# Modulation columns by TensorE, x loaded first, and unread products between the first transposes

## Chip, cores and metric

One Trainium2 chip, one of its cores. The metric is the device time of the whole program in microseconds (us). Times inside the program come from one profiled execution of it.

## What is computed

Two layers of a diffusion backbone over 1024 latent and 256 context tokens of width 1024, all in float32. Every sub-layer normalizes its input and modulates it with a shift and a scale that are worked out from a conditioning vector:

```python
mod_lat = (silu_c @ ada_w[i] + ada_b[i])[:, None, :]
sh1, sc1, g1, sh2, sc2, g2 = jnp.split(mod_lat, 6, axis=-1)
h = modulate(rms_norm(x, norm_g[i, 0]), sh1, sc1)        # h * (1 + sc1) + sh1
y = chunk_mlp(h, a_w_in[j], ...)                         # layer 0: gelu(h @ w_in), gating, @ w_out
x = x + g1 * rms_norm(y, norm_g[i, 1])
h = modulate(rms_norm(x, norm_g[i, 2]), sh2, sc2)
x = x + g2 * rms_norm(conv_ffn(h, ...), norm_g[i, 3])
```

Layer 1 has windowed attention in the place of `chunk_mlp`. The change touches only the first line above and the two behind it, for layer 0 and the first five latent tiles: `sh1`, `sc1`, the normalization, and the first quarter of `h @ w_in`.

## The kernel before

Tokens are handled in tiles of 128. The first pass takes five latent tiles (`LAT`). Its start, the **head**, is written out by hand at the end of the quoted code: the instructions of VectorE (`V`), ScalarE (`S`), TensorE (`T`) and the DMA queue of SyncE (`Q`) between `pins.update` and `pins.clear` stay in the order in which they are written. Instructions behind the head, and those of POOL (`G`), are placed by a scheduler.

The head works through the width of 1024 in eight **chunks** of 128 columns. For each chunk k:

- the shift and scale of the chunk are needed as two **columns** of 128 values. `AdaBlock` loads that slice of `ada_w` (two halves of 1024 x 128 for one chunk, or x 256 for two chunks), `accum` multiplies its eight row blocks by the conditioning vector and sums them on VectorE, `total` sums over partitions with products with ones on TensorE, and `finish` adds the bias and the norm's weight (three small operations on VectorE);
- `flip_x(k)` transposes the five scaled tiles of x into a psA bank (five transposes). The scaling (`rstd_of` and the line behind it) takes a square on ScalarE, two small operations on POOL and one scaling on VectorE for each tile;
- `x_hi(k)` applies the columns on ScalarE (two `ACTIVATE`) and casts the result to the high part (one `CAST`); `x_lo(k)` takes the low part on VectorE;
- `w_load`, `w_hi`, `w_lo` load a tile of `w_in` for two chunks and split it in the same way;
- `head_mm(k, part)` is one **group** of five products of 128x512; three parts for each chunk, 24 groups in all, accumulate in four psB banks and one psA bank.

The blocks are one chunk wide for chunks 0 and 1 and two wide for 2-3, 4-5 and 6-7. Loaded slices sit in six `act` buffers, weight tiles in three `raw` buffers. Behind the head the raw buffers are a **ring** that weight tiles of `w_in` and rows of `ada_w` for the next modulations take in turn: a load starts when the tile before it in its buffer has been read by VectorE. There are two psA banks; during the head one of them holds a sum of products. Behind the head, transposes for `lncols` and the two `cwcols` (constants for later) go through psA too, and VectorE copies them out.

At profile time nearly every instruction carries line 50, that of a helper which records all operations, so instructions are told apart by engine and by the tiles that they write and read (`psB<-wh,big`: a product into a psB tile from a weight's high part and a big tile).

Of the kernel before, what the change touches and what calls it, by code (L numbers as in the profile page):

```python
# [10 lines left out]
F32 = mybir.dt.float32  # L11
# [4 lines left out]
P = 128  # L16
D = 1024
KD = D // P
# [14 lines left out]
def hybrid_kernel(  # L33
# [164 lines left out]
    def finish_cols(l, m, s, p, ks):  # L198
        dst = mod_cols(l, m, s)[:, ks]
        V.tensor_tensor(out=dst, in0=p, in1=abcols[:, 48 * l + 8 * m:48 * l + 8 * m + 8][:, ks], op=ALU.add)  # L200
        if m in (1, 4):
            o = 32 * l + (0 if m == 1 else 16)
            V.scalar_tensor_tensor(out=dst, in0=dst, scalar=1.0, in1=ngcols[:, o:o + 8][:, ks],
                                   op0=ALU.add, op1=ALU.mult)
# [122 lines left out]
    def src_row(stage, t):  # L327
        if stage == 0:
            return x_in[0, t * P:(t + 1) * P, :] if t < 8 else ctx_in[0, (t - 8) * P:(t - 7) * P, :]
        return xs[stage][t * P:(t + 1) * P, :]  # L330
# [254 lines left out]
    pA0 = psA()  # L585
    pl0 = [psB() for _ in range(4)] + [pA0[:, 0, :]]

    class AdaBlock:
        def __init__(self, k0, nk):
            self.k0, self.nk = k0, nk  # L590
# [28 lines left out]
                             start=True, stop=True)  # L619

        def finish(self):
            k0, nk = self.k0, self.nk
            p = pts[k0][:, 1, 256:256 + 2 * nk]
            for s in (1, 0):
                finish_cols(0, s, 0, p[:, s * nk:(s + 1) * nk], slice(k0, k0 + nk))

    raws, w0, pts, tms = {}, {}, {}, {}

    def w_load(u, nb=0):
        raws[nb, u] = t_raw()  # L630
        Q.dma_start(raws[nb, u].rearrange("p (a b) -> p a b", a=2),
                    w_in[0][u * 256:u * 256 + 2 * P, E + nb * 512:E + nb * 512 + 512]
                    .rearrange("(k p) n -> p k n", p=P))

    def w_hi(u, nb=0):
        hi, lo = t_w("wh"), t_w("wl")
        w0[nb, u] = (hi.rearrange("p (a b) -> p a b", a=2), lo.rearrange("p (a b) -> p a b", a=2))
        S.copy(hi, raws[nb, u])
        raws[nb, u] = (raws[nb, u], hi, lo)

    def w_lo(u, nb=0):
        raw, hi, lo = raws.pop((nb, u))
        V.tensor_sub(lo, raw, hi)

    def flip_x(k):
        pts[k] = psA()
        for i in range(5):
            T.transpose(out=pts[k][:, i // 4, (i % 4) * P:(i % 4 + 1) * P], in_=xn0[:, i, k * P:(k + 1) * P],
                        identity=ident)

    def x_hi(k):
        pt, tm = pts[k], t_tmp()
        gg, sh = mod_cols(0, 1, 0)[:, k:k + 1], mod_cols(0, 0, 0)[:, k:k + 1]
        S.activation(tm[:, 0:512], pt[:, 0, :], AF.Identity, bias=sh, scale=gg)
        S.activation(tm[:, 512:640], pt[:, 1, 0:128], AF.Identity, bias=sh, scale=gg)
        S.copy(hk(hb0, 0, k)[:, 0:640], tm[:, 0:640])
        tms[k] = tm

    def x_lo(k):
        V.tensor_sub(hk(hb0, 1, k)[:, 0:640], tms[k][:, 0:640], hk(hb0, 0, k)[:, 0:640])  # L660
# [12 lines left out]
        V.tensor_copy(cl, p)  # L673
        return cl

    b0 = AdaBlock(0, 1)
    adab, aR = load_rows([ada_b.rearrange("l (k p) -> (l k) p", p=P)])
    ngr, nR = load_rows([norm_g.rearrange("l i (k p) -> (l i k) p", p=P)])
    for i, t in enumerate(LAT):
        Q.dma_start(xn0[:, i, :], src_row(0, t))  # L680
    w_load(0)
    b1 = AdaBlock(1, 1)
    abcols = cols_in(adab, aR, "abcols")
    ngcols = cols_in(ngr, nR, "ngcols")
    b0.accum(range(KD))
    for i, t in enumerate(LAT):
        r = rstd_of(xn0[:, i, :])
        V.tensor_scalar(out=xn0[:, i, :], in0=xn0[:, i, :], scalar1=r, scalar2=None, op0=ALU.mult)
    flip_x(0)
    b0.total()  # L690
    w_hi(0)
    b0.finish()
    x_hi(0)
    w_lo(0)
    flip_x(1)
    b1.accum(range(0, 4))
    x_lo(0)
    b2 = AdaBlock(2, 2)
    head_mm(0, 0)
    b1.accum(range(4, 8))  # L700
    b1.total()
    b2.accum(range(0, 2))
    b1.finish()
    head_mm(0, 1)
    head_mm(0, 2)
    x_hi(1)
    b2.accum(range(2, 4))
    w_load(1)
    b3 = AdaBlock(4, 2)
    flip_x(2)  # L710
    x_lo(1)
    w_hi(1)
    b2.accum(range(4, 7))
    head_mm(1, 0)
    head_mm(1, 1)
    w_lo(1)
    b2.accum(range(7, 8))
    b2.total()
    head_mm(1, 2)
    b3.accum(range(0, 1))  # L720
    b2.finish()
    x_hi(2)
    b3.accum(range(1, 3))
    x_lo(2)
    w_load(2)
    b4 = AdaBlock(6, 2)
    flip_x(3)
    x_hi(3)
    b3.accum(range(3, 5))
    x_lo(3)  # L730
    w_hi(2)
    head_mm(2, 0)
    head_mm(2, 1)
    head_mm(2, 2)
    flip_x(4)
    head_mm(3, 0)
    b3.accum(range(5, 7))
    w_lo(2)
    b3.accum(range(7, 8))
    head_mm(3, 1)  # L740
    b3.total()
    b4.accum(range(0, 1))
    b3.finish()
    head_mm(3, 2)
    x_hi(4)
    b4.accum(range(1, 3))
    x_lo(4)
    w_load(3)
    flip_x(5)
    x_hi(5)  # L750
    b4.accum(range(3, 5))
    x_lo(5)
    head_mm(4, 0)
    head_mm(4, 1)
    head_mm(4, 2)
    flip_x(6)
    w_hi(3)
    head_mm(5, 0)
    head_mm(5, 1)
    b4.accum(range(5, 8))  # L760
    b4.total()
    w_lo(3)
    b4.finish()
    head_mm(5, 2)
    x_hi(6)
    x_lo(6)
    w_load(0, 1)
    flip_x(7)
    x_hi(7)
# [1351 lines left out]
```

## Time and profile before

| what | us |
|---|---|
| median of three runs | 2856.6 |
| lowest and highest of them | 2850.05, 2860.5 |
| profiled execution, its own time | 2860.88 |
| span of the profiled execution | 2859.1 |

| first 66 us of that execution | us |
|---|---|
| first product of the head | 23.08 |
| last product of the head | 65.07 |

In the timeline a row has the start in us, the duration, the engine, the line, the operation with its output and inputs, how many such instructions were merged, and in brackets how long the engine stood idle before it and what released it. A merged row's duration runs from the first start to the last end. Ends of products are modelled, so the pitch of two starts is the better measure of their cost.

### The profile page before, as it was taken

Reading aid. Unit: us, or ns where it says so; the run is one execution under the profiler, and the core shown is the slowest. Engines: PE = TensorE matmul, PEld = TensorE weight load, DVE = VectorE, ACT = ScalarE, POOL = GpSimd, SP = SyncE. Lnnn points to the kernel's source line nnn. Section 1 sums busy time; section 2 is a strip of 40 time slices with the busy share of each in tenths; the row PEclk is TensorE's granted clock in tenths of the full one; section 3 lists DMA queues with packets and bytes.
Section 4 is the critical chain, followed back from the end, with each engine's and each line's share of the span. In section 5 each row is a group of like instructions: output and inputs, shape, how many; then the busy total and the mean of one; then the engine's idle time right before and its main releaser. Section 6 shows DMA issues by size and latency. Waiting matters only on the chain.

```text
span 2859.1 us, 40314 instructions
## 1 busy us (share of the span) xinstructions
PE 2741.8 (96%) x14570; PEld 2354.1 (82%) x14570; DVE 2221.8 (78%) x3466; ACT 1391.2 (49%) x2291; POOL 616.6 (22%) x806
## 2 busy tenths in 40 slices
PE   7999999999989999999999899999998999999998
PEld 5798887898889888888788778888887888888786
DVE  6567684787779899887776568898887788888776
ACT  4333242232367444455434545777876444445433
POOL 1164021360210212111000124543333121220000
PEclk9999999999999999999999999999999999999999
DMA  7775457554488355467855565347577345545753
GB/s 260 251 234 166 145 161 227 177 167 131 171 249 240 103 170 162 157 217 238 287 169 184 188 212 186 115 145 239 181 242 220 126 162 182 160 144 198 248 177 125
DMA packets 436335, 537.13 MB, mean 188 GB/s; under 512 B 20004, under 2 KB 300452, under 8 KB 436135
## 3 DMA queue, kind: packets, MB, share of 16 engines
q1 hardware_dynamic: 379575, 470.84, 51.4%
q10 hardware_dynamic: 55408, 59.52, 6.2%
q0 software_dynamic: 1152, 4.19, 0.4%
q8 instruction: 115, 1.88, 0.3%
q14 instruction: 85, 0.70, 0.1%
HBM read 414.40 MB, written 120.07 MB: 187 GB/s over the span
## 4 chain that ended last, share of the span: by engine, by line
PE 65%; DVE 13%; DMA 11%; ACT 5%; issue 4%; POOL 2%; SPq 1%; ACTq 0%; DVEq 0%; POOLq 0%
PE psB L50 48%; PE psA L50 16%; DVE row L50 3%; DVE wl L50 3%; DMA raw<-in_ada_w_dram 3%; DVE tmp L50 1%; DVE acc L50 1%; ACT wh L50 1%; ACT tmp L50 1%; DMA xT<-row 1%; DMA raw<-in_a_w_in_dram 1%; DVE y L50 1%; POOL sm L50 1%; DMA raw<-in_f_w_up_dram 1%; DMA raw<-in_f_w_down_dram 1%
## 5 line engine op out<-in xcount | busy, mean ns | idle before, releaser
L50 PE MATMUL psB<-cmb,wh 128*128 128x512 f32 (+2 forms) x2584 | 750.3, 374 | 7.2 <-ACT row L50 6.2
L50 PEld LDWEIGHTS psB<-cmb,wh 128*128 128x128 f32 x2584 | 471.9, 188 | 98.4 <-ACT row L50 8.1
L50 PE MATMUL psB<-cmb,wl 128*128 128x512 f32 (+2 forms) x1292 | 483.2, 374 | 0.2 <-DVE wl L50 0.2
L50 ACT CAST wh<-raw 128x1024 fp32r<-128x1024 f32 (+1 forms) x313 | 265.1, 863 | 441.6 <-PE psB L50 165.5
L50 DVE TENSOR_TENSOR wl<-raw,wh 128x1024 fp32r<-128x1024 f32 (+1 forms) x313 | 307.6, 997 | 106.6 <-ACT wh L50 104.9
L50 PEld LDWEIGHTS psB<-cmb,wl 128*128 128x128 f32 x1292 | 243.2, 188 | 44.0 <-DVE wl L50 0.8
L50 PE MATMUL psB<-wh,big 128*128 128x512 f32 x816 | 271.1, 398 | 3.7 <-ACT big L50 1.3
L50 ACT CAST wh<-row 128x1024 fp32r<-128x1024 f32 (+1 forms) x196 | 162.5, 834 | 186.8 <-DVE row L50 92.3
L50 PE MATMUL psB<-wh,act 128*128 128x512 f32 x640 | 200.1, 390 | 0.8 <-DVE tmp L50 0.8
L50 DVE TENSOR_TENSOR wl<-row,wh 128x1024 fp32r<-128x1024 f32 (+1 forms) x196 | 185.2, 948 | 12.2 <-ACT wh L50 11.8
L50 PE MATMUL psA<-big,wh 128*128 128x320 f32 x1024 | 193.2, 310 | 0.3 <-ACT row L50 0.3
L50 POOL TENSOR_TENSOR row<-raw,raw 128x512 f32<-128x512 f32 x44 | 68.5, 1558 | 574.2 <-DMA raw<-in_f_w_up_dram 490.8
L50 PEld LDWEIGHTS psB<-wh,big 128*128 128x128 f32 x816 | 154.3, 190 | 39.9 <-ACT tmp L50 2.4
L50 DVE SCALAR_TENSOR_TENSOR acc<-raw,ccols,acc 128x1024 f32<-128x1024 f32 x98 | 126.7, 1311 | 75.8 <-DMA raw<-in_ada_w_dram 75.5
L50 DVE SCALAR_TENSOR_TENSOR row<-row,cwcols,row 128x1024 f32<-128x1024 f32 (+2 forms) x142 | 152.6, 1075 | 39.2 <-ACT row L50 22.7
L50 ACT CAST ah<-raw 128x1024 fp32r<-128x1024 f32 x80 | 77.6, 974 | 201.6 <-PE psB L50 80.8
L50 DVE TENSOR_TENSOR row<-row,row 128x512 f32<-128x512 f32 (+4 forms) x169 | 155.9, 926 | 19.9 <-DMA row<-actd 12.2
L50 POOL TENSOR_SCALAR row<-row,sm,sm 128x128 f32<-128x128 f32 x160 | 144.1, 919 | 115.2 <-DMA row<-vscr 99.3
L50 PEld LDWEIGHTS psA<-big,wh 128*128 128x128 f32 x1024 | 159.9, 188 | 0.7 <-ACT row L50 0.5
L50 PE MATMUL psB<-wl,big 128*128 128x512 f32 x408 | 157.2, 395 | 0.9 <-DVE wl L50 0.9
L50 DVE TENSOR_TENSOR al<-raw,ah 128x1024 fp32r<-128x1024 f32 x80 | 90.2, 1128 | 71.9 <-ACT ah L50 71.6
L50 PE MATMUL psB<-row,wh 128*128 128x256 f32 x744 | 136.9, 286 | 8.2 <-ACT wh L50 6.7
(279 smaller groups left out, 6226.0 us busy)
## 6 DMA issues: line engine op xcount, KB each, us to landing
raw<-in_f_w_up_dram SPq DMA_DIRECT2D x121, 512.0 KB, 4.8
raw<-in_ada_w_dram SPq DMA_DIRECT2D x88, 512.0 KB, 4.4
raw<-in_a_w_in_dram SPq DMA_DIRECT2D x64, 512.0 KB, 4.8
wh<-woscr SPq DMA_DIRECT2D x48, 512.0 KB, 4.1
row<-actd SPq DMA_DIRECT2D x44, 512.0 KB, 5.5
actc<-row SPq DMA_DIRECT2D x44, 512.0 KB, 4.1
raw<-actc SPq DMA_DIRECT2D x40, 512.0 KB, 3.6
actd<-row SPq DMA_DIRECT2D x39, 512.0 KB, 2.7
```

The costliest lines, as they stand in the source:

```text
L50: ins = fn(*a, **kw)
```

## The change

`AdaBlock` for chunks 0 and 1, and the first half of the block of 2-3, give way to four `AdaColumn`. An `AdaColumn` loads the two slices of one chunk in two DMAs of 512 KB and needs no sums on VectorE: `total` makes each of the two columns by eight products that accumulate, with the slice as the stationary operand and a column of the conditioning vector as the moving one. Chunks 4-5 and 6-7 keep `AdaBlock`. The loads of x move ahead of the first modulation columns. Three products of ones, whose result is not read, stand ahead of each of the five transposes of chunk 0. The cast of the first weight tile is cut in two halves and moves behind `x_hi(0)`. The written order of the head changes with all this.

```diff
+    class AdaColumn:
+        def __init__(self, k0):
+            self.k0, self.nk, self.rv = k0, 1, {}
             for s in (1, 0):
+                self.rv[s] = t_act((P, KD, P), F32)
+                Q.dma_start(self.rv[s], ada_w[0, :, s * D + k0 * P:s * D + (k0 + 1) * P]
+                            .rearrange("(k p) n -> p k n", p=P))
+
+        def total(self):
+            p = pts[self.k0][:, 1, 256:258]
+            for s in (1, 0):
+                for k in range(KD):
+                    T.matmul(p[:, s:s + 1], self.rv[s][:, k, :], ccols[:, k:k + 1], start=(k == 0), stop=(k == KD - 1))
...
-        S.copy(hi, raws[nb, u])
+        for c in ((0, 512), (512, 1024)) if (nb, u) == (0, 0) else ((0, 1024),):
+            S.copy(hi[:, slice(*c)], raws[nb, u][:, slice(*c)])
...
         for i in range(5):
+            for _ in range(3 if k == 0 else 0):
+                T.matmul(pA0[:, 1, :], ones_r, ones_r.unsqueeze(1).to_broadcast([P, 4, P]), start=True, stop=True)
             T.transpose(out=pts[k][:, i // 4, (i % 4) * P:(i % 4 + 1) * P], in_=xn0[:, i, k * P:(k + 1) * P],
...
-    b0 = AdaBlock(0, 1)
     adab, aR = load_rows([ada_b.rearrange("l (k p) -> (l k) p", p=P)])
     ngr, nR = load_rows([norm_g.rearrange("l i (k p) -> (l i k) p", p=P)])
     for i, t in enumerate(LAT):
         Q.dma_start(xn0[:, i, :], src_row(0, t))
+    b0 = AdaColumn(0)
     w_load(0)
-    b1 = AdaBlock(1, 1)
+    b1 = AdaColumn(1)
+    b2 = AdaColumn(2)
...
-    b0.accum(range(KD))
...
     b0.total()
-    w_hi(0)
     b0.finish()
     x_hi(0)
+    w_hi(0)
+    x_lo(0)
     w_lo(0)
+    b3 = AdaColumn(3)
+    w_load(1)
+    head_mm(0, 0)
     flip_x(1)
...
+    b4.accum(range(4, 8))
+    w_hi(2)
     flip_x(4)
     head_mm(3, 0)
-    b3.accum(range(5, 7))
+    head_mm(3, 1)
+    b4.total()
+    b4.finish()
+    x_hi(4)
     w_lo(2)
...
     flip_x(5)
     x_hi(5)
-    b4.accum(range(3, 5))
     x_lo(5)
+    b6.accum(range(2, 5))
     head_mm(4, 0)
     head_mm(4, 1)
     head_mm(4, 2)
     flip_x(6)
     w_hi(3)
+    b6.accum(range(5, 8))
     head_mm(5, 0)
+    b6.total()
+    b6.finish()
+    x_hi(6)
+    w_lo(3)
+    x_lo(6)
     head_mm(5, 1)
-    b4.accum(range(5, 8))
-    b4.total()
-    w_lo(3)
-    b4.finish()
     head_mm(5, 2)
-    x_hi(6)
-    x_lo(6)
```

Three places as the built programs have them. First POOL at the start of the program; `mask` is a constant for the attention of layer 1, `sm` and `rstT` are the two small operations of each tile's scaling. Before:

```order
L50 MEMSET lead_194 128x16
L50 MEMSET mask 128x640
L50 AFFINE_SELECT mask<-mask 128x384 x2
L50 TENSOR_SCALAR sm_157<-sm_157 128x1
L50 TENSOR_TENSOR rstT<-sm_157,mhalf 128x1
L50 TENSOR_SCALAR sm_163<-sm_163 128x1
L50 TENSOR_TENSOR rstT<-sm_163,mhalf 128x1
```

And now:

```order
L50 TENSOR_SCALAR sm_147<-sm_147 128x1
L50 MEMSET lead_221 128x16
L50 MEMSET mask 128x640
L50 TENSOR_TENSOR rstT<-sm_147,mhalf 128x1
L50 AFFINE_SELECT mask<-mask 128x384
L50 TENSOR_SCALAR sm_153<-sm_153 128x1
L50 TENSOR_TENSOR rstT<-sm_153,mhalf 128x1
L50 AFFINE_SELECT mask<-mask 128x384
L50 TENSOR_SCALAR sm_159<-sm_159 128x1
```

The mask's four operations moved from ahead of the first tile to between the first three.

Second VectorE at the end of the head, around the columns of chunks 6 and 7: `acc` are sums of `accum`, `big` low parts of x (chunks 4, 5, 6), `wl` the low part of the last weight tile, `modc` the three operations of `finish`. Before:

```order
L50 TENSOR_TENSOR big_413<-tmp_406,big_409 128x640
L50 SCALAR_TENSOR_TENSOR acc_341<-act_332,ccols,acc_341 128x512
L50 SCALAR_TENSOR_TENSOR acc_341<-act_335,ccols,acc_341 128x512
L50 TENSOR_TENSOR big_413<-tmp_423,big_409 128x640
L50 SCALAR_TENSOR_TENSOR acc_341<-act_335,ccols,acc_341 128x512
L50 SCALAR_TENSOR_TENSOR acc_341<-act_338,ccols,acc_341 128x512 x2
L50 TENSOR_TENSOR wl_452<-raw_415,wh_451 128x1024
L50 TENSOR_TENSOR modc<-psA_445,abcols 128x2
```

And now:

```order
L50 TENSOR_TENSOR big_450<-tmp_439,big_442 128x640
L50 TENSOR_SCALAR acc_361<-act_349,ccols 128x512
L50 SCALAR_TENSOR_TENSOR acc_361<-act_349,ccols,acc_361 128x512
L50 TENSOR_TENSOR big_450<-tmp_462,big_442 128x640
L50 SCALAR_TENSOR_TENSOR acc_361<-act_352,ccols,acc_361 128x512 x2
L50 SCALAR_TENSOR_TENSOR acc_361<-act_355,ccols,acc_361 128x512 x2
L50 SCALAR_TENSOR_TENSOR acc_361<-act_358,ccols,acc_361 128x512 x2
L50 TENSOR_TENSOR modc<-psA_485,abcols 128x2
L50 SCALAR_TENSOR_TENSOR modc<-modc,ngcols 128x2
L50 TENSOR_TENSOR modc<-psA_485,abcols 128x2
L50 TENSOR_TENSOR wl_492<-raw_454,wh_491 128x1024
```

All eight sums of these columns now stand behind the low part of chunk 4, six of them in a row behind that of chunk 5, where five stood behind the one, three of these behind the other; the weight's low part moved from ahead of `finish` to behind it.

Third VectorE in the stage behind the head, around the copies of `cwcols`. Rows with `acc` and `raw` read one row block of `ada_w` for the next modulations (eight make one modulation; a new one begins with `TENSOR_SCALAR`); `st` are statistics of the stage's first results. Before:

```order
L50 SCALAR_TENSOR_TENSOR acc_608<-raw_827,ccols,acc_608 128x1024
L50 SCALAR_TENSOR_TENSOR acc_608<-raw_885,ccols,acc_608 128x1024
L50 COPY cwcols_696<-psA_694 128x66
L50 TENSOR_TENSOR wl_833<-raw_830,wh_832 128x1024
L50 TENSOR_SCALAR acc_942<-raw_943,ccols 128x1024
L50 BN_STATS st_538<-tmp_752 128x6
L50 BN_STATS st_538<-tmp_756 128x6
L50 BN_STATS st_538<-tmp_760 128x6
L50 COPY cwcols_739<-psA_737 128x66
```

And now:

```order
L50 SCALAR_TENSOR_TENSOR acc_648<-raw_867,ccols,acc_648 128x1024
L50 COPY cwcols_736<-psA_734 128x66
L50 TENSOR_TENSOR wl_873<-raw_870,wh_872 128x1024
L50 SCALAR_TENSOR_TENSOR acc_648<-raw_925,ccols,acc_648 128x1024
L50 BN_STATS st_578<-tmp_792 128x6
L50 BN_STATS st_578<-tmp_796 128x6
L50 BN_STATS st_578<-tmp_800 128x6
L50 COPY cwcols_779<-psA_777 128x66
L50 TENSOR_SCALAR acc_982<-raw_983,ccols 128x1024
```

The first read of the second modulation, the ninth read in all, moved from ahead of the second copy to behind it; each copy has one read less ahead of it.

More of the change, by code (lines that the diff above doesn't have):

```diff
@@ L586, in hybrid_kernel, with finish_block @@
     pl0 = [psB() for _ in range(4)] + [pA0[:, 0, :]]
+    def finish_block(block):
+        k0, nk = block.k0, block.nk
+        p = pts[k0][:, 1, 256:256 + 2 * nk]
+        for s in (1, 0):
+            finish_cols(0, s, 0, p[:, s * nk:(s + 1) * nk], slice(k0, k0 + nk))
     class AdaBlock:
@@ L621, in finish @@
         def finish(self):
-            k0, nk = self.k0, self.nk
-            p = pts[k0][:, 1, 256:256 + 2 * nk]
+            finish_block(self)
+    class AdaColumn:
+        def __init__(self, k0):
+            self.k0, self.nk, self.rv = k0, 1, {}
             for s in (1, 0):
-                finish_cols(0, s, 0, p[:, s * nk:(s + 1) * nk], slice(k0, k0 + nk))
+                self.rv[s] = t_act((P, KD, P), F32)
[3 more added lines that the diff above has]
+            p = pts[self.k0][:, 1, 256:258]
+            for s in (1, 0):
+                for k in range(KD):
+                    T.matmul(p[:, s:s + 1], self.rv[s][:, k, :], ccols[:, k:k + 1], start=(k == 0), stop=(k == KD - 1))
+        def finish(self):
+            finish_block(self)
     raws, w0, pts, tms = {}, {}, {}, {}
@@ L690, in hybrid_kernel @@
     b0.total()
-    w_hi(0)
     b0.finish()
     x_hi(0)
+    w_hi(0)
+    x_lo(0)
     w_lo(0)
+    b3 = AdaColumn(3)
+    w_load(1)
+    head_mm(0, 0)
     flip_x(1)
[L696 to L700, printed above, removed]
     b1.total()
-    b2.accum(range(0, 2))
     b1.finish()
+    x_hi(1)
     head_mm(0, 1)
     head_mm(0, 2)
[L706 to L709, printed above, removed]
+    x_lo(1)
+    b4 = AdaBlock(4, 2)
     flip_x(2)
-    x_lo(1)
+    b2.total()
+    b2.finish()
+    x_hi(2)
     w_hi(1)
-    b2.accum(range(4, 7))
+    b4.accum(range(0, 2))
     head_mm(1, 0)
     head_mm(1, 1)
+    head_mm(1, 2)
+    x_lo(2)
     w_lo(1)
[L717 to L724, printed above, removed]
     w_load(2)
-    b4 = AdaBlock(6, 2)
+    b6 = AdaBlock(6, 2)
     flip_x(3)
+    b3.total()
+    b3.finish()
     x_hi(3)
-    b3.accum(range(3, 5))
-    x_lo(3)
-    w_hi(2)
+    b4.accum(range(2, 4))
     head_mm(2, 0)
@@ L734, in hybrid_kernel @@
     head_mm(2, 2)
+    x_lo(3)
+    b4.accum(range(4, 8))
+    w_hi(2)
     flip_x(4)
     head_mm(3, 0)
-    b3.accum(range(5, 7))
+    head_mm(3, 1)
+    b4.total()
+    b4.finish()
+    x_hi(4)
     w_lo(2)
[L739 to L743, printed above, removed]
     head_mm(3, 2)
-    x_hi(4)
-    b4.accum(range(1, 3))
     x_lo(4)
+    b6.accum(range(0, 2))
     w_load(3)
```

## Prediction

> **What bounds the kernel now.** I read the page first, then the timeline of the first 66 us (the stretch that the edit rewrites), then the chain of waits behind it.
>
> ```profile
> span 2859.1 us, 40314 instructions
> PE 2741.8 (96%) x14570; PEld 2354.1 (82%) x14570; DVE 2221.8 (78%) x3466; ACT 1391.2 (49%) x2291; POOL 616.6 (22%) x806
> PE   7999999999989999999999899999998999999998
> ```
>
> TensorE is busy 96% of the span. Only the first of 40 slices (71 us each) stands at 7, and the whole edit lies in it. A gain or a loss there moves everything behind it by as much, unless a later wait takes it up, so that wait has to be looked for too. The 0.5% below (14.3 us), about what a measurement of this kernel can tell from no change, is a fifth of that slice.
>
> The road to the first big product, from the timeline:
>
> ```profile
> 1.47 0.63 POOL L50 MEMSET mask<- 128x640 f32 x1
> 1.52 2.05 SPq L50 DMA_DIRECT2D act<-in_ada_w_dram  x4
> 2.17 1.08 POOL L50 TENSOR_SCALAR_AFFINE_SELECT mask<-mask 128x384 f32<-128x384 f32 x2
> ...
> 9.23 3.61 DVE L50 SCALAR_TENSOR_TENSOR acc<-act,ccols,acc 128x256 f32<-128x256 f32 x7
> 9.96 1.06 ACT L50 ACTIVATE tmp<-y 128x1024 bf16<-128x1024 f32 x1 [5.60 <-DMA y<-in_x_dram]
> ...
> 17.17 0.75 DVE L50 TENSOR_SCALAR y<-y,rstT 128x1024 f32<-128x1024 f32 x1 [0.71 <-POOL rstT L50]
> ...
> 18.05 0.55 POOL L50 TENSOR_TENSOR rstT<-sm,mhalf 128x1 f32<-128x1 f32 x1
> 18.63 0.75 DVE L50 TENSOR_SCALAR y<-y,rstT 128x1024 f32<-128x1024 f32 x1 [0.71 <-POOL rstT L50]
> ...
> 19.71 0.85 PE L50 MATMUL psA<-ones,acc 128*128 128x1 f32 x4
> ...
> 21.14 1.13 ACT L50 ACTIVATE tmp<-psA,modc 128x512 f32<-128x512 f32 x2 [2.94 <-DVE modc L50]
> ...
> 22.30 0.72 ACT L50 CAST big<-tmp 128x640 fp32r<-128x640 f32 x1
> ...
> 23.08 2.08 PE L50 MATMUL psB<-wh,big 128*128 128x512 f32 x4 [1.34 <-ACT big L50]
> ```
>
> x lands at 9.96. Its five tiles are then scaled at a pitch of 1.46 us (17.17 to 18.63): POOL's power and VectorE's scaling wait for each other. Column sums, modulation and cast follow, and the first product starts at 23.08, at about 0.5 us each: a slow clock, though the page's granted clock says full. The rest of the head:
>
> ```profile
> 31.94 0.71 PE L50 MATMUL psA<-ident,y 128*128 128x128 f32 x5
> ...
> 32.40 1.18 PE L50 MATMUL psB<-wh,big 128*128 128x512 f32 x4
> ...
> 38.66 1.20 PE L50 MATMUL psB<-wh,big 128*128 128x512 f32 x4
> ...
> 39.38 1.53 DVE L50 SCALAR_TENSOR_TENSOR acc<-act,ccols,acc 128x512 f32<-128x512 f32 x2
> ...
> 53.65 1.22 DVE L50 TENSOR_TENSOR wl<-raw,wh 128x1024 fp32r<-128x1024 f32 x1
> ...
> 54.90 0.33 SPq L50 DMA_DIRECT2D raw<-in_ada_w_dram  x1
> 54.90 0.95 PE L50 MATMUL psA<-ones,acc 128*128 128x1 f32 x8
> 55.71 1.19 PE L50 MATMUL psB<-wl,big 128*128 128x512 f32 x4
> ...
> 60.31 0.82 DVE L50 TENSOR_TENSOR big<-tmp,big 128x640 fp32r<-128x640 f32 x1 [0.50 <-ACT big L50]
> ...
> 61.90 1.07 PE L50 MATMUL psB<-wh,big 128*128 128x512 f32 x4
> ...
> 63.03 1.07 PE L50 MATMUL psB<-wh,big 128*128 128x512 f32 x4
> ...
> 65.07 0.39 PE L50 MATMUL psA<-wl,big 128*128 128x512 f32 x1
> ```
>
> A group of five products takes 1.13 us at full clock (61.90 to 63.03), five transposes 0.46 (31.94 to 32.40), eight one-column products 0.81 (54.90 to 55.71), a sum on VectorE 0.765 (1.53 for two). Chunk 2 starts at 38.66; the last product of the head starts at 65.07, and the next stage 0.23 later, at 65.3.
>
> Behind the head one wait is large. The chain of waits, then the timeline:
>
> ```profile
> 92.70 5.08 DMA raw<-in_ada_w_dram
> 97.80 0.75 DVE acc L50
> ```
>
> ```profile
> 100.26 0.21 DVE L50 COPY cwcols<-psA 128x66 f32<-128x66 f32 x1
> 100.52 0.79 PE L50 MATMUL psA<-wh,big 128*128 128x512 f32 x1 [4.58 <-DVE cwcols L50]
> 101.11 0.63 PE L50 MATMUL psA<-wl,big 128*128 128x512 f32 x1
> 101.54 0.63 PE L50 MATMUL psA<-wh,big 128*128 128x512 f32 x1
> ...
> 103.84 0.63 PE L50 MATMUL psB<-wh,big 128*128 128x512 f32 x2
> ```
>
> TensorE stands from 95.94 (100.52 less 4.58) to 100.52 for a psA bank. The copy that frees it is queued on VectorE behind a read of a modulation tile that lands only at 97.80, through the ring of three raw buffers. After the wait, products come every 0.43 us until about 103.6.
>
> **The change, part by part.** Terms are against the profiled execution (2860.88 us; 2859.1 of it is the span). It lies 4.3 above the median 2856.6, and the sum is carried over to the median as a difference.
>
> *First product: +0.3.* The four ada_w issues (2.05 us) and their 1.05 MB leave the way of x, whose first tile I put at 7.8, an estimate from those 2.05 us and the 9.96. But POOL now sets the mask (0.63) between the first tile's two operations, and does half of its 1.08 ahead of each of the next two. With the pitch of 1.46 unchanged, the last scaling ends about 17.85 instead of 19.38. Then 16 one-column products stand where 4 took 0.85: 1.6 at full clock, about 3.4 at the slow one (0.85 for four). At full clock they end at about 20.0 to 20.3. From there the old steps count: 0.58 to the modulation (20.56 to 21.14), 1.13, 0.73, and now half a weight cast (512 columns: 0.55, an estimate from the 0.72 of 640) that used to lie earlier, under cover. First product at 23.35 against 23.08. Dropping VectorE's first sums gains nothing here: they were done while x loaded.
>
> *Up to chunk 2: from -1.6 to 0.* From first product to chunk 2 TensorE has six groups (6.8), three flips (1.4) and three times 16 one-column products (5.1, between twice 0.81 and twice 0.92): 13.3 us. The loads, from the view of DMA between 5 and 20 us:
>
> ```profile
> DMA packets 4613, 5.13 MB, mean 342 GB/s; under 512 B 240, under 2 KB 3717, under 8 KB 4613
> ```
>
> At 0.342 MB a microsecond, with 512-byte pieces as the new columns have them, the 6.3 MB of x, one weight tile and three columns take 18.4 us, so the third column lands about 24, four before it is needed. So chunk 2 at 36.65, were the clock full throughout. But between column sums and first product TensorE stands still for about 3.1 us (0.58 + 1.13 + 0.73 + 0.55 and latencies). What gaps do to the clock, from the timeline:
>
> ```profile
> 1394.86 0.50 PE L50 MATMUL psA<-wh,ah 128*128 128x512 f32 x1 [2.76 <-ACT s L50]
> 1395.20 0.40 PE L50 MATMUL psA<-wl,ah 128*128 128x512 f32 x1
> ```
>
> ```profile
> 2149.05 0.79 PE L50 MATMUL psA<-wh,row 128*128 128x512 f32 x1 [2.89 <-ACT row L50]
> 2149.64 0.63 PE L50 MATMUL psA<-wl,row 128*128 128x512 f32 x1
> 2150.06 0.63 PE L50 MATMUL psA<-wh,row 128*128 128x512 f32 x1
> ```
>
> After 2.76 us of idling the pace stayed full; after 2.89 and 4.58 it fell to 0.43 per product. For 3.1 us I take slow, the nearer row: about 3.1 us at half pace (100.52 to 103.6), 1.6 lost. Chunk 2 at 38.25; both ends are kept.
>
> The Trainium skill (TensorE: Matmul & The Clock Gate, Part 1) says that the clock drops only after a whole idle window of about 3.4 us, and that the window runs free. By that rule a 3.1 us gap keeps the clock and chunk 2 stands at 36.65; the 2.89 row speaks against it.
>
> *Chunk 2 to the end of the head: +0.8.* VectorE is lighter by 14 us in all (16 sums of 0.5, by the row at 9.23, and 8 of 0.765), but the sums left stand later in its queue. Counting from chunk 2: the modulation and cast of chunk 3 end at 2.5, its low part (0.82) at 3.3, four sums at 6.4; TensorE gets there at 6.1. Totals 0.85, then modulation and cast of chunk 4 to 9.7. Now VectorE has, in order, a low part, two sums, a low part, six sums: 0.82 + 1.23 + 0.82 + 4.6, so 17.2. TensorE, with four groups and a flip, is there at 14.7: **a new wait of 2.5 us** for the last columns, where before it had none (54.90). Totals 0.9, then eight groups and a flip, 9.5: the head ends 27.6 after chunk 2, at 65.85 (64.25 with the clock kept), against 65.3.
>
> *Behind the head: -4.1 in all.* The last weight split (53.65 to 54.87) now stands behind those columns, and ends 19.8 after chunk 2: at 58.05, 3.2 later. It frees the raw buffer from which the ring goes on (54.90). Yet the second copy of cwcols now stands behind the eighth modulation read instead of the ninth: one hop less, 5.1 + 0.75. So 100.26 + 3.2 - 5.85 = 97.6. TensorE arrives at 95.94 + 0.55 = 96.5, waits some 1.3 and goes on at about 97.9 instead of 100.52: -2.7. A wait that short leaves the clock alone; seven products at 0.43 instead of 0.226 fall away: -1.4. A hop is the least certain of these: the ring's DMA rows on the chain run from 3.64 to 6.75 us, so the whole lies between -5.4 (TensorE does not wait at all) and +3.2 (no hop saved).
>
> From there on every engine's order is as before and TensorE is busy nearly all the time, so I carry the difference to the end: 2860.9 - 4.1 = 2856.8 for the profiled execution, **2852.5** on the scale of the median. That is 0.14%: no change by the bound above.
>
> **The rivals.**
> - *The clock survives the gap.* Chunk 2 at 36.65, the split 1.6 late, the copy at 96.0: -4.3 - 1.4, so 2850.9. For it: the 2.76 row, and the rule of the skill named above. Against it: the 2.89 row.
> - *Slower: the ring takes it all.* The late split holds back every later load by 3.2, and the saved hop is eaten because the eighth read now follows three weight tiles through one raw buffer, where it followed two (raw_652, raw_741 and raw_817 ahead of raw_925; before, raw_701 and raw_777 ahead of raw_885). Copy at 103.5, TensorE going on at 103.7 with a slow clock: +3.2, 2859.8. It decides from the moment that the copy comes later than 101.9 (100.26 plus the 1.4 of the clock and a little). For it: the row at 92.70, where the chain waits for nothing but the ring. Against: one read less stands before the copy.
> - *The unread products do not bring the clock up.* Three at 0.5 us and a transpose take longer than the pitch of 1.46 and hold the transposes back; last transpose at 19.2, column products slow, first product at 26.2, chunk 2 at 41.1, head end 68.7, split 60.9, copy 100.4, and TensorE goes on at 100.7 without a lost clock: -1.2, 2855.4. For it: ten transposes and four column products up to 21.7 left the clock slow. Against: 512 columns of plain product, back to back, are what ran before 31.94, where it rose.
>
> None of these reaches 14.3 us: TensorE's own work from the first product on is 37 us of the head (24 groups, 7 flips, 5.1 and 1.7 of columns), so an end before 60 is out of reach, and the wait behind it is worth 6 at most.
>
> **How the numbers follow.** Forecast 0.42, clock kept 0.18, slower ring 0.22, no warming 0.10, something else 0.08. The three runs shown spread by 10 us, so a median moves by some 3 of itself. 2846 to 2862 takes in all four times with that spread. Beyond 0.5% only the unnamed cases reach: faster 0.03, slower 0.03, same 0.94.
>
> **What would show it.** In the timeline of the changed kernel: x's first square near 7.8; last scaling ending near 17.9; first product near 23.4, at 0.43 per product (0.226 if the clock was kept); chunk 2 near 38; the two unbroken sums of chunks 6 and 7 followed by an idle TensorE of 2 to 3 us before eight one-column products; head end near 66; the copy of cwcols near 97.6 and a wait of under 2 us. I am wrong if the first product comes before 21, if TensorE does not wait for the last sums, or if the wait near 97 is as long as before.

## The result, and the profile after

| kernel | median, us | runs | lowest to highest | ratio to before, 95% interval |
|---|---|---|---|---|
| before | 2851.07 | 6 | 2846.16 to 2860.5 | |
| changed | 2869.99 | 6 | 2869.0 to 2873.49 | 1.0064 [1.0046, 1.0082] |

The change makes the kernel slower by 0.64%, some 19 us. The prediction, 2852.5 and no change, was wrong. The profiled execution of the changed kernel has a span of 2867.4 us.

The timeline of TensorE in the head of the changed kernel. `psA<-ccols,act` are the new column products:

```profile
16.32 3.95 PE L50 MATMUL psA<-ccols,act 128*128 128x1 f32 x32
23.30 2.07 PE L50 MATMUL psB<-wh,big 128*128 128x512 f32 x4 [3.03 <-ACT wh L50]
...
26.49 3.89 PE L50 MATMUL psA<-ccols,act 128*128 128x1 f32 x32
...
34.49 3.63 PE L50 MATMUL psA<-ccols,act 128*128 128x1 f32 x32
...
42.06 3.63 PE L50 MATMUL psA<-ccols,act 128*128 128x1 f32 x32
45.55 1.16 PE L50 MATMUL psB<-wh,big 128*128 128x512 f32 x4
46.55 0.41 PE L50 MATMUL psA<-wh,big 128*128 128x512 f32 x1
46.78 1.90 PE L50 MATMUL psB<-wh,big 128*128 128x512 f32 x4
48.47 0.63 PE L50 MATMUL psA<-wh,big 128*128 128x512 f32 x1
...
64.41 1.05 PE L50 MATMUL psA<-ones,acc 128*128 128x1 f32 x8 [2.04 <-DVE acc L50]
...
74.87 0.39 PE L50 MATMUL psA<-wl,big 128*128 128x512 f32 x1
75.10 0.39 PE L50 MATMUL psA<-wh,big 128*128 128x512 f32 x1
```

Two things are to be seen. The count: the program writes 16 column products for a chunk, the trace has 32, so each is two instructions, and a chunk's columns take 3.63 us at best (0.113 for one instruction) where the old ones took 0.81 for two chunks. And the pace: four products take 1.16 us at 45.55 and 1.90 us at 46.78, with no idle time between. The next stage starts at 75.10; before, at 65.3.

Behind the head, one row from each of several timelines of the changed kernel (VectorE, SyncE, TensorE, SyncE, ScalarE, TensorE):

```profile
65.84 1.22 DVE L50 TENSOR_TENSOR wl<-raw,wh 128x1024 fp32r<-128x1024 f32 x1
...
67.08 0.33 SPq L50 DMA_DIRECT2D raw<-in_ada_w_dram  x1
...
107.79 0.50 PE L50 MATMUL psA<-wh,big 128*128 128x512 f32 x1 [0.91 <-DVE cwcols L50]
...
128.12 0.90 SPq L50 DMA_DIRECT2D row<-in_x_dram  x2
...
134.71 1.06 ACT L50 ACTIVATE tmp<-row 128x1024 bf16<-128x1024 f32 x1 [10.51 <-DMA row<-in_x_dram]
...
138.37 3.08 PE L50 MATMUL psB<-ones,acc 128*128 128x1 f32 x16 [4.77 <-ACT tmp L50]
```

and the same steps at the reload before:

```profile
116.77 0.90 SPq L50 DMA_DIRECT2D row<-in_x_dram  x2
...
124.00 1.06 ACT L50 ACTIVATE tmp<-row 128x1024 bf16<-128x1024 f32 x1 [8.89 <-DMA row<-in_x_dram]
...
127.67 1.95 PE L50 MATMUL psB<-ones,acc 128*128 128x1 f32 x16
```

The ring's first load is issued at 67.08 instead of 54.90. The wait for cwcols shrinks from 4.58 to 0.91, and TensorE's lag behind the first profile of before from 9.8 (75.10 against 65.3) to 7.3 (107.79 against 100.52). Then a wait stands where none was: rows of x are loaded once more for the next tiles, on SyncE behind the ring's loads; ScalarE squares them (the row at 134.71), and the gelus that free psB stand behind these squares in its order; the first of them starts at 137.75. TensorE waits 4.77, and the lag is 10.7 (138.37 against 127.67). The views of waits of the two, 60 to 180 us, before and then changed:

```profile
PE psA L50 <- DVE cwcols L50: 4.6, 1, 4.6
```

```profile
PE psB L50 <- ACT tmp L50: 5.3, 2, 4.8
PE psA L50 <- DVE acc L50: 2.0, 1, 2.0
PE psA L50 <- DVE cwcols L50: 0.9, 1, 0.9
```

The spans differ by 8.3, less than the medians: a second profile of before (below) spans 2851.2, so the first was a long execution. I use that second one, called the reference, for lags: how much later the same product starts. In the changed kernel the lag is 8.1 at 80 us (on the reference's time), 3.5 at 126, 11.7 at 135 and 16.2 at the end. From 135 to 2200 it stays between 9.9 and 12.8, and only then rises. Two executions of one kernel drift like that too: the first profile of before is 0.6 ahead of the reference at 145 and 7.9 behind it at the end. So this last rise is not put down to the change.

### The profile page after: what moved, and what is told of

Read it like the earlier page. It is cut to its first block, busy times and chain, and to the rows that moved or that the text cites. A ratio compares the mean times of both kernels' runs of the same rounds, so it can differ in the third digit from the quotient of the medians.

```text
span 2867.4 us, 40529 instructions
## 1 busy us (share of the span) xinstructions
PE 2757.4 (96%) x14697; PEld 2368.5 (83%) x14697; DVE 2208.4 (77%) x3445; ACT 1390.5 (48%) x2292; POOL 622.7 (22%) x806
## 4 chain that ended last, share of the span: by engine, by line
PE 62%; DVE 13%; DMA 12%; issue 5%; ACT 5%; POOL 2%; SPq 1%; ACTq 0%; DVEq 0%; POOLq 0%
PE psB L50 46%; PE psA L50 17%; DVE row L50 4%; DMA raw<-in_ada_w_dram 3%; DVE wl L50 3%; DVE acc L50 1%; DVE tmp L50 1%; DMA xT<-row 1%; ACT wh L50 1%; ACT tmp L50 1%; DMA raw<-in_f_w_up_dram 1%; DMA raw<-in_a_w_in_dram 1%; DMA row<-xT 1%; DVE y L50 1%; DMA row<-actd 1%
```

## The experiments

Ratios are to the kernel before, run beside each.

| run | what | median, us | ratio, 95% interval |
|---|---|---|---|
| e1_no_ones | changed, without the unread products | 2876.19 | 1.0085 [1.0066, 1.0105] |
| e2_sums_on_vector | changed, with all sums on VectorE | 2871.27 | 1.0065 [1.0049, 1.0082] |
| e3_split_early | changed, last weight split earlier | 2874.99 | 1.0073 [1.0057, 1.009] |
| e4_before_again | before | 2852.6 | 0.9996 [0.9986, 1.0007] |
| f1_x_first | before, with x loaded first | 2852.22 | 0.9994 [0.9983, 1.0005] |
| f2_before_ones | before, with the unread products | 2856.65 | 1.001 [0.9995, 1.0025] |
| f3_reload_pool | changed, reload of x by POOL | 2870.71 | 1.0063 [1.0041, 1.0085] |
| f4_half_columns | changed, half of the column products | 2864.22 | 1.0033 [1.0021, 1.0045] |
| g1_ones_between | changed, unread products between columns | 2886.84 | 1.0116 [1.0103, 1.0129] |
| g2_fill_gap | changed, unread products in the first gap | 2876.68 | 1.0083 [1.0068, 1.0097] |
| g3_reload_again | f3 once more | 2875.31 | 1.0076 [1.006, 1.0092] |
| g4_before_scalar | before, copies by ScalarE, reload by POOL | 2855.93 | 1.0003 [0.9994, 1.0013] |
| h1_one_column | changed, one product for each column | 2855.62 | 1.0006 [0.9997, 1.0014] |
| h2_one_column_reload | h1, reload of x by POOL | 2850.03 | 0.9994 [0.9985, 1.0002] |
| h3_after_again | changed, once more | 2874.79 | 1.0076 [1.0062, 1.0091] |
| i1_split_runs | changed, columns in two stretches | 2876.23 | 1.009 [1.0076, 1.0104] |
| i2_split_runs_reload | i1, reload of x by POOL | 2872.94 | 1.0074 [1.006, 1.0088] |

### Undoing one part

```diff
-            for _ in range(3 if k == 0 else 0):
+            for _ in range(0):
```

> The changed kernel without the fifteen unread products of ones; all else as it was. Theory A (the sixteen column products of a chunk are 32 instructions and 3.6 to 4 us of TensorE, and these are what the change pays): the ones cost nothing, as they lie under the scaling of x; the last transpose ends at about 16.3 as before, the first column products run at the slow clock and take 4.5 to 7 instead of 3.95 us, so the time rises by 0 to 3 us (2870 to 2873). Rival B (the unread products hold the transposes back or do not bring the clock up): the time falls by 1 to 3 us.

Without the unread products the first two sets of columns run at half pace, as the timeline of TensorE shows:

```profile
16.61 6.83 PE L50 MATMUL psA<-ccols,act 128*128 128x1 f32 x32
26.47 2.08 PE L50 MATMUL psB<-wh,big 128*128 128x512 f32 x4 [3.03 <-ACT wh L50]
...
29.83 6.83 PE L50 MATMUL psA<-ccols,act 128*128 128x1 f32 x32
```

Without them the median is 1.4 to 6.2 us higher than that of the changed kernel (second or first series). The intervals overlap, so a saving is not shown, but they make no part of the loss. That 6.83 us of column products at half pace did not bring the pace up is the first sign that they count for little there.

```diff
-    b0 = AdaColumn(0)
+    b0 = AdaBlock(0, 1)
...
+    b0.accum(range(KD))
     flip_x(0)
     b0.total()
```

(the same for chunks 1 to 3)

> The changed kernel with the columns of chunks 0 to 3 made as before (sums on VectorE, two products with ones), each chunk's eight sums placed just ahead of its totals; x first, the unread products and the order of the rest stay. Theory A: TensorE loses four times 3.6 us of column products and gets four times about 0.45 back; VectorE's eight sums of 0.5 us now bound chunks 0 to 2, so the head ends at 66 to 70 instead of 75.1 and the time falls by 5 to 10 us (2860 to 2865). Rival C (the order of the last sums and splits on VectorE, and with it the late start of the ring, is what costs): the head may shorten, but the waits behind it take it back and the time stays within 3 us of 2870.

No gain: in place of the column products TensorE waits for VectorE's sums ahead of all four totals (3.57, 2.12, 2.04 and 2.92 us). In this order of loads and steps VectorE is late too, so undoing the columns this way tells nothing of their cost. The time is the one that rival C foresaw; h1 below, which keeps the order, tells the two apart.

```diff
     w_hi(3)
+    w_lo(3)
     b6.accum(range(5, 8))
...
-    w_lo(3)
```

> The changed kernel with the split of the head's last weight tile placed ahead of the last three sums of chunks 6 and 7, as before, so that the ring starts earlier (67.08 in the changed kernel). The last sums end 1.2 us later for it. Theory A alone: TensorE is late by itself, the head ends at 75 to 77, and the time stays within 3 us of 2870. Rival C (the late ring start causes the waits near 107 and 138): the first load of the ring is issued near 63, the wait of 4.8 us near 138 goes, and the time falls by 4 to 7 us.

The ring now started 14.5 us ahead of the head's end (8.0 in the changed kernel), and the wait near 138 did not come. But the wait for cwcols was back (4.4), the wait for the last sums grew to 3.0, and the head ended 19.1 later than in the reference. The wait moves with the ring's start, as supposed, and the time does not gain, because this head is 11.0 longer than that of the changed kernel's first profile: three of its four sets of columns ran below full pace. From 80 to 145 us the lag rises by 0.1 here, and by 3.6 in the changed kernel. So behind the head the early split is worth some 3.5 us, which the head hides.

> The kernel before, unchanged, for a second profile of it. Its first profiled execution took 2860.9 while the median of six runs is 2851.1; the changed kernel's first profile is only 8.3 us longer in span. If the runs of before differ by chance in some stage, this profile shows a shorter span and in which stage; the head is expected to be the same to 0.5 us (last product at 65.1), and the ratio 1.000 within 0.003.

This is the reference: the wait for cwcols is 4.8 in it. The span is shorter, as expected, by 7.9, but the head is not the same to 0.5: x is there later (first square at 11.88 instead of 9.96), the first product comes at 24.31 instead of 23.08, and the next stage starts at 66.96, 1.66 later. What made the first execution long lies behind the head.

```diff
-    b0 = AdaBlock(0, 1)
...
         Q.dma_start(xn0[:, i, :], src_row(0, t))
+    b0 = AdaBlock(0, 1)
```

> The kernel before with one edit: the five loads of x stand ahead of the first modulation slices; all sums stay on VectorE. Theory 1 (the order of the loads costs): x's first square comes about 1.5 us earlier, but the eight sums of chunk 0 now wait for slices behind x, the columns are late as in the run with all sums on VectorE (first product 24.4 there, 23.1 before), and the time is that of before plus 1 to 3 us. Theory 2 (x is what the first product waits for): first product near 21.5 and before minus 1 to 2 us. Either way under 4 us, so the loads' order alone does not make the 16 to 19 us of the change.

x's first square comes at 6.38, yet the first product only at 24.02 (23.08 and 24.31 in the two profiles of before), since the sums of chunk 0 stand ahead of x's scaling on VectorE and wait for their slices until 13.02. The time shows no difference: the loads' order alone costs nothing that can be measured.

```diff
         for i in range(5):
+            for _ in range(3 if k == 0 else 0):
+                T.matmul(pA0[:, 1, :], ones_r, ones_r.unsqueeze(1).to_broadcast([P, 4, P]), start=True, stop=True)
```

(in the kernel before)

> The kernel before with one edit: three unread products of ones ahead of each of chunk 0's five transposes. Theory 1 (the idle gap of about 3 us in front of the first product takes the clock away again): transposes are quicker, the first product stays within 0.5 us of 23.1 and runs at half pace, time within 3 us of before. Theory 2 (the raised clock lasts into the first groups): the first 20 to 25 products at 0.226 instead of 0.43 us, head end 4 us earlier and 2 to 4 us off the time.

The head's first product comes at 23.38, and from 27.27 on the pace is full, but TensorE then waited 2.33 for a sum and fell back; the time is as before. Alone the unread products neither gain nor cost that can be measured, and the column products are left.

### The size of the column products

```diff
-                for k in range(KD):
+                for k in range(0, KD, 2):
```

> The changed kernel with half of the column products of chunks 0 to 3 left out (row blocks 0, 2, 4 and 6 of the modulation weights only, so shift and scale of these chunks are those of half the sum): 32 program products, or 64 instructions, fewer. Theory 1 (the double instructions lengthen the head): 4 times 1.8 us less in the head, 7 us; the ring starts 5 to 7 us earlier, and the time is 5 to 8 us below the changed kernel, near 2863. Theory 2 (late sums and the written order set the head, the columns lie beside them): head end and time change by under 2 us.

```diff
-                for k in range(KD):
+                for k in range(0, KD, 8):
```

> The changed kernel with all column products of chunks 0 to 3 but one for each column left out (row block 0 of the modulation weights only): four instructions for each chunk where there were 32. Theory 1 (the double instructions, and the clock that falls during them, are what lengthens the head): no product behind the first groups at 0.43 us, head end 9 to 13 us earlier than in the changed kernel (where the last sums, on VectorE, then hold it), and the time near 2857 to 2860: half the products gave 2864.2. Theory 2 (the remaining loss is the order and the ring's late start): head end stops at that of the half, 2.3 us behind the unchanged kernel, and the time stays at 2863 to 2865.

With 2, 8 and 16 program products for a chunk the medians are 2855.62, 2864.22 and 2869.99 (2874.79 in the second series): from 2 to 8 is 24 products and 8.6 us, from 8 to 16 is 32 and 5.8 to 10.6 us. These medians are of different series; h1 and the second series of the changed kernel ran beside each other and differ by 19.2. So nearly the whole loss goes with the column products and with what they do to the pace. In the timeline of h1 the head has no slow group from 26.16 on, and its next stage starts at 60.93, 14.2 ahead of the changed kernel:

```profile
27.84 0.50 PE L50 MATMUL psA<-ccols,act 128*128 128x1 f32 x4
28.20 1.17 PE L50 MATMUL psB<-wh,big 128*128 128x512 f32 x4
...
50.23 1.05 PE L50 MATMUL psA<-ones,acc 128*128 128x1 f32 x8 [2.04 <-DVE acc L50]
...
60.71 0.39 PE L50 MATMUL psA<-wl,big 128*128 128x512 f32 x1
60.93 0.39 PE L50 MATMUL psA<-wh,big 128*128 128x512 f32 x1
```

Of these 14.2, four times 3.13 (3.63 less 0.50) are the products themselves, 12.5; the rest is pace. The wait for the last sums is the same 2.04 here: it does not make the difference. That h1 is as fast as before is a sum of two: its lag behind the reference is -6.0 at 80 us and -9.9 at 106, and the reload's wait, 5.4 here, brings it to -1.4.

### The pace

> The changed kernel unchanged, beside the two above. Theory 1 (the clock falls during the column products in a number of places that differs from execution to execution): a median of 2870 to 2876, a spread of 8 us or more, and a head in the profile that need not have the one fall of the first profile. Theory 2 (the head always runs as in the first profile): median within 2 us of 2870, spread of 5 us, the same pitch at each group.

The same program, another execution; rows of its timeline of TensorE:

```profile
34.58 0.71 PE L50 MATMUL psA<-ident,y 128*128 128x128 f32 x5
35.12 4.33 PE L50 MATMUL psA<-ccols,act 128*128 128x1 f32 x32
39.31 2.05 PE L50 MATMUL psB<-wh,big 128*128 128x512 f32 x4
...
45.34 0.71 PE L50 MATMUL psA<-ident,y 128*128 128x128 f32 x5
45.88 4.80 PE L50 MATMUL psA<-ccols,act 128*128 128x1 f32 x32
50.55 2.05 PE L50 MATMUL psB<-wh,big 128*128 128x512 f32 x4
...
82.14 0.39 PE L50 MATMUL psA<-wh,big 128*128 128x512 f32 x1
```

Both sets start at full pace (the five transposes ahead of them take 0.54), slow down within the 4 us, and the groups behind run at half pace for some 5 us. This head ends at 82.14, 7.0 later than in the first profile, where only one of these two falls was seen: of the kernel's 20 us, 2 to 9 are pace, by chance of the execution.

The traces also hold the granted clock. The view of windows gives it for any stretch. In these rows of the changed kernel's first profile, the figures are the stretch and its length, TensorE's busy time and instructions, the granted clock (1.00 or 0.50), and two of the DMA:

```profile
16.06:19.47 3.41, 3.41 (x32) 1.00 1.15 347
19.47:22.88 3.41, 0.80 (x5) 0.50 1.15 347
...
26.30:29.71 3.41, 3.41 (x33) 1.00 0.07 17
29.71:33.12 3.41, 3.41 (x11) 0.50 0.86 284
...
43.36:46.78 3.42, 3.42 (x27) 1.00 0.46 149
46.78:50.19 3.41, 3.41 (x10) 0.50 0.89 257
```

So the pace is the clock: it falls to half at 19.47, 29.71 and 46.78, after stretches in which TensorE was busy throughout, and comes back at 26.30, 33.12 and 50.19. (The record starts with the rise at 16.06; ahead of its first change the view reads 1.00 at half pace too, which is why the page of the profile showed a full clock there.) In each of the nineteen traces all changes lie a multiple of 3.413 us apart, and where this grid begins differs from execution to execution.

The Trainium skill (TensorE: Matmul & The Clock Gate, Part 1) says that the clock is judged over a window of about 3.4 us which runs free of the program, so that the same kernel measures differently; the grid and the two executions agree with that. It also says that the clock drops after an idle window; here it dropped after windows without a gap, and the measurement decides: one-column products did not hold the clock.

```diff
                     T.matmul(p[:, s:s + 1], self.rv[s][:, k, :], ccols[:, k:k + 1], start=(k == 0), stop=(k == KD - 1))
+                    if k % 4 == 3:
+                        T.matmul(pA0[:, 1, :], ones_r, ones_r.unsqueeze(1).to_broadcast([P, 4, P]), start=True, stop=True)
```

> The changed kernel with one unread product of ones behind every four column products (four for each chunk, 0.9 us at full clock). Theory 1 (one-column products count as idleness and let the clock fall): no product of 512 columns behind the column products of chunks 2 and 3 runs at 0.43 us, as ten did from 46.78 in the changed kernel; 3.6 us of added work against about 2 to 6 us of clock, so the time is 2867 to 2872. Theory 2 (the clock falls there by chance or for another reason): slow products stay behind those columns, and the time is 3 to 4 us above 2870.

Further off than either theory has it: 12 to 17 us slower than the changed kernel's two series. One plain product in 0.81 us of columns does not hold the pace (timeline of TensorE):

```profile
40.74 0.95 PE L50 MATMUL psA<-ccols,act 128*128 128x1 f32 x8
41.54 0.48 PE L50 MATMUL psA<-ones 128*128 128x512 f32 x1
41.86 1.08 PE L50 MATMUL psA<-ccols,act 128*128 128x1 f32 x8
42.80 0.77 PE L50 MATMUL psA<-ones 128*128 128x512 f32 x1
43.38 1.70 PE L50 MATMUL psA<-ccols,act 128*128 128x1 f32 x8
```

Eight instructions go from 0.8 to 1.6 us on the way.

```diff
     b0.total()
+    for _ in range(10):
+        T.matmul(pA0[:, 1, :], ones_r, ones_r.unsqueeze(1).to_broadcast([P, 4, P]), start=True, stop=True)
```

> The changed kernel with ten unread products of ones behind the column products of chunk 0, in the 3 us in which TensorE waits for the first high part. Theory 1 (that gap takes the clock): the first product stays near 23.3, the groups of chunk 0 and 1 run at 0.226 instead of 0.43 us, chunk 2's first group comes 3 to 4 us earlier, and the time is 2 to 4 us below 2870. Theory 2 (the column products before and behind it take the clock anyway): first groups at 0.43 still, time within 1.5 us of 2870.

The pace fell before the gap, during the columns; the ten products then ran at half pace (4.61 us) and held the first group back to 25.09. It fell again during each of the next three sets of columns. The median is no better (the interval overlaps that of the changed kernel's second series): the gap of 3.03, which I took for the place where the pace is lost, is not what loses it.

```diff
-    b2.total()
-    b2.finish()
-    x_hi(2)
+    b2.total((1,))
     w_hi(1)
-    b4.accum(range(0, 2))
     head_mm(1, 0)
+    b2.total((0,))
+    b2.finish()
+    x_hi(2)
+    b4.accum(range(0, 2))
```

(chunks 1 and 3 alike)

> The changed kernel with the same column products, but those of chunks 1 to 3 in two halves with a group of five products of the chunk before between them: no stretch of one-column products longer than 1.9 us at full clock. Theory 1 (a long stretch of one-column products lets the clock fall, whatever its count): groups behind the columns of chunks 2 and 3 at full pace, 1.13 us each; the direct 12.5 us of the products stay, up to 8 of the clock go, so the time is 2865 to 2869, with a narrower spread than the 9 us of the changed kernel. Theory 2 (the clock falls with the number of such products, or at random): groups at half pace behind them as before, time 2870 to 2875.

A miss. Stretches of 1.84 us with a group of 1.13 between still lost the pace in chunks 1 and 2 and kept it in chunk 3. So the length of one stretch is not what counts. What the runs agree with is the share of plain products over a few us: half the columns between the same groups (f4) showed no fall behind the columns of chunks 2 and 3. The clock's grid gives the share. Over the first 90 us of the nineteen traces, take each step of 3.41 us that runs at full clock, and add up the time of its products of 512 columns. All 25 steps with less than 0.79 us end with a fall, and all 213 with more than 1.57 us keep the clock. Of the 42 between, half fall; what decides there stays open. So it is a matter of where the grid cuts the columns, and one plain product between eight instructions (g1) or one group between two halves (i1) leaves steps below 1.57.

### The wait at the reload

```diff
-                Q.dma_start(xr[n], src_row(0, MIX[n]))
+                if n < 2:
+                    G.tensor_copy(xr[n][:, 0:1], cols["lng"][:, 0:1])
+                (G if n < 2 else Q).dma_start(xr[n], src_row(0, MIX[n]))
```

(the copy only holds the load back until lncols is there; the order on TensorE, VectorE and ScalarE is unchanged)

> The changed kernel with one edit: the two loads that fetch the first reloaded rows of x are issued by POOL, once lncols is copied (near 94), instead of by SP behind the ring's loads (near 128); the order on TensorE, VectorE and ScalarE stays. Theory 1 (the debt is given back at the reload): the square comes when ScalarE reaches it, TensorE's wait of 4.8 us near 138 goes, the lag behind the unchanged kernel stays at 3 to 5 us from 126 on, and the time is 6 to 8 us below that of the changed kernel, near 2863. Theory 2 (the ring, or something else, holds TensorE there): the wait stays under another name and the time stays within 2 us of 2870.

> The kernel that loads the reloaded x by POOL once more: its wait near 138 was gone, but its profiled execution had lost 9.8 us more in the head, at a low clock, than that of the changed kernel, and its five runs lay between 2865.7 and 2878. Theory 1 (the reload costs 6 to 8 us, and the low clock in the head was that execution's own): a head end within 2 us of the changed kernel's, no wait near 138, a median near 2864 to 2866. Theory 2 (the low clock in the head comes with this kernel): head end late again and a median of 2870 or more.

In both profiles the wait near 138 is gone: the lag stays at 14.6 and at 15.3 from 126 to 135, where the changed kernel's rises by 8.2. But both heads had fallen to half pace with three sets of columns (lags of 17.9 and 18.4 at 80), and the medians gain nothing. With h1's short columns, whose head keeps its pace, the same edit does show:

> The kernel with one product for each column, and besides the two reloads of x issued by POOL behind lncols. With the columns short the head's clock is the same in both, so the difference of the two is the reload alone. Theory 1 (the wait at the reload is real time): the wait of TensorE near 130 goes and the time is 5 to 7 us below the other. Theory 2 (what the profiles showed there is given back further on, as two runs of the full kernel with this edit hint, at 2870.7 and 2875.3): the two times lie within 2 us of each other.

5.6 us less than the run beside it (the intervals against before still meet at their edges; drawing anew from the twelve times of each gives a difference of 1.7 to 7.3). The views of waits, h1 and then h2, 50 to 180 us:

```profile
PE psB L50 <- ACT tmp L50: 6.2, 2, 5.4
PE psA L50 <- DVE acc L50: 2.0, 1, 2.0
PE psA L50 <- DVE cwcols L50: 0.9, 1, 0.9
```

```profile
PE psA L50 <- DVE acc L50: 2.0, 1, 2.0
PE psA L50 <- DVE cwcols L50: 1.6, 1, 1.6
PE psB L50 <- ACT tmp L50: 1.2, 1, 1.2
```

> The same with the two reloads of x issued by POOL behind lncols. Theory 1 (with the clock steady the reload shows in the time as it did with one product for each column, 5.6 us): 5 to 7 us below the run beside it, near 2861, and still above before by the columns' own 7 to 10 us. Theory 2 (the reload is worth nothing where the columns are long): within 2 us of the run beside it.

3.3 us less than i1 beside it, with intervals that overlap. The profiles say more than these medians, as the lag leaves the head out. From 80 to 145 us it rises by 2.1 to 4.8 in the nine profiles with the late split and the reload on SyncE (the changed kernel twice, e1, e2, f4, g1, g2, h1, i1), and falls by 1.4 to 3.0 in the four with the reload by POOL (f3, g3, h2, i2). At 300 us the means are +4.7 and -0.4. So the reload's wait is real time, some 5 us, as h2 has it. It does not show in the medians of f3 and g3, whose profiled heads were 10 us longer than that of the changed kernel's first profile: the chances of the heads are larger than the effect.

```diff
-        V.tensor_copy(cols, p[:, :R])
+        (S.copy if wide else V.tensor_copy)(cols, p[:, :R])
```

(in the kernel before, with the reload by POOL)

> The kernel before with two edits: the copies of lncols and of both cwcols are made by ScalarE, where they stand behind fewer ring steps than on VectorE, and the two reloads of x are issued by POOL behind lncols. Theory 1 (TensorE's waits near 96 and 130 are two ends of one debt to the ring, and with both ends off the ring nothing else is late): the wait of 4.8 us for cwcols goes, none comes in its place, and with the clock kept behind it the time is 4 to 6 us below before, near 2849. Theory 2 (the ring itself feeds TensorE there): the wait turns up behind another name, for a weight or an acc, within 40 us, and the time is within 2 us of before.

In the profile the wait for cwcols is gone; one of 2.6 for `row` comes instead, and the span is 2846.3. The median shows none of it. With h2, this is as near as a run came to a version better than both kernels: h2 leaves out seven eighths of the column products and so computes something else, and its interval still takes in no change.

## Why the prediction was wrong

**First product: right, by two errors.** Forecast 23.35, measured 23.30. x's first square came at 6.30, 1.5 earlier than the 7.8, and the columns took 3.95 instead of 1.6. The gap and the slow first groups behind it came as forecast, but the gap did not slow them: in this profile the clock fell at 19.47, while the columns ran, and the gap began at 20.27. The grid also tells apart the two rows of the prediction that seemed to set a limit: it cuts the gap of 2.76 into two steps with 1.78 and 2.29 us of products of 512 columns, and the gap of 2.89 lies in one step with 1.33.

**"Up to chunk 2: from -1.6 to 0": this step failed, by a term's size.** I took "three times 16 one-column products" as 5.1, with a price from rows that read x4 and x8. Those rows count instructions, and an `AdaBlock` of one chunk writes two products, not four: they showed the factor of two, and I read it as the program's count. Measured: 10.7 (26.49 to 30.24, 34.49 to 37.98, 42.06 to 45.55), so 5.6 more. With 1.7 more of half pace than forecast, chunk 2 came at 45.55 instead of 38.25. h1 and f4 bear the size out.

**"Chunk 2 to the end of the head: +0.8": nearly right.** Forecast 27.6 us, measured 29.55; the wait for the last sums 2.5 against 2.04. Of the 1.95 more, some 1.6 are the slow groups from 46.78: TensorE came to the totals of chunk 4 at 53.53, 7.98 after chunk 2, where I had 6.4. I had a fall of the pace only after idle gaps; the runs show it during the columns too. The rival on unread products that do not bring the pace up did not come true: they did, and e1 shows what it costs without them.

**"Behind the head: -4.1": right in kind.** One hop was saved, TensorE waited 0.91 (forecast 1.3), and the lag to the reference fell from 8.1 at 92 to 3.5 at 126. The rival with the whole ring late by 3.2 had the right sign, but put the price at the cwcols copy.

**"From there on ... I carry the difference to the end": failed.** I looked for the next wait on the ring at the copy alone. The reload of x is issued 60 to 63 us after the ring's first load in before, reference, changed kernel, e1, e2 and h1 alike (66.9 in e3), so a ring that starts 12.2 later is late there whatever was won on the way: 4.77 at 138. Against TensorE the ring is later by 2.4, as it starts 8.0 ahead of the head's end instead of 10.4. In h1 it is 8.0 as well, with a wait of 5.4, and in e3 it is 14.5, with none: this part comes from where the split stands, not from the columns. Both steps count: the mis-sized term with its pace made 9 us of the head, the reload took back 8 of lag.

The base was off too: 2856.6 was the median of three runs, and six give 2851.07. Against its base the forecast said -4.1, and the measured difference is +18.9. The two steps are 17 of these 23 us; for the rest no step is shown.

## What to carry to other kernels

Count instructions on both sides: hold the trace's x-number of a row against the number of calls in the code before a duration is taken from it. Products with one moving column cost their own time and can take the pace from the wide products behind them, without an idle gap to see; the granted clock over stretches of a few us shows it. A wait that shrinks early is a gain only when the next engine fed by the same late queue has been looked at too.

## What was not expected of the hardware

- A float32 product with one moving column is two instructions, 0.113 us each at full pace and 0.213 at half (3.63 and 6.83 us for 32).
- The granted clock changed only on a grid of 3.413 us, placed differently in each execution. It fell during one-column products without idle time, at other places in two executions of one program (heads of 75.1 and 82.1). Fifteen plain products of 512 columns, three for each transpose, brought it up; 6.83 us of one-column products did not.
- Medians of one program moved by 4.8 us between two series (2869.99, 2874.79), so an effect of 5 us needs its own partner beside it.
